# Two pads that move the large tiles of both ends of the on-chip memory to multiples of 512 bytes, and one rotation buffer less

## The chip, the cores and the metric

The kernel runs on one core of a Trainium2 chip. The core has TensorE (PE; its weight loads are shown apart, as PEld), VectorE (DVE), ScalarE (ACT), GpSimd (POOL) and SyncE (SP, which issues the DMAs). Its on-chip memory has 128 partitions; a tile takes the same range of bytes in each of them, and an address below is a byte offset within a partition. The metric is the device time of one execution, in microseconds (us).

## The reference

One inference step of a one-layer hybrid encoder, in float32, for 1024 new frames of one stream (the prompt) and 16 frames for each of 8 running streams (the samples), 1152 rows in all. After an RMSNorm one input projection feeds two groups of heads: a gated linear recurrence (RG-LRU) and a sparse attention whose keys are chosen by an indexer's top-k. Both meet in an output projection, and a SwiGLU feed-forward of width 2816 follows.

```python
h = rmsnorm(x, norm_mix);  proj = h @ w_in            # xr, gate, q, k, v, qi, ki, wi
xc, conv_new = causal_conv(xr, conv_prev, conv_w, conv_b)
hs, h_last = rglru(xc, pos, h_prev, ...);  y_a = hs * gelu(gate)
q = rope(rmsnorm(q, q_norm), pos);  k = rope(rmsnorm(k, k_norm), pos)
qi = rope(qi, pos);  ki = rope(ki, pos)
topk = min(256, k_all.shape[1] // 4)
y_b = dsa_attend(q, qi, wi, pos, k_all, v_all, ki_all, k_pos, topk)
x = x + concatenate([y_a, y_b], -1) @ w_out
gu = rmsnorm(x, norm_ffn) @ w_ffn_in
x = x + (silu(gu[..., :2816]) * gu[..., 2816:]) @ w_ffn_out
```

## The kernel before

The 1152 rows are nine tiles of 128. Every operand of a large product is split into a high and a low part, and a product is three matmuls (`mm3`, L245): low weights by high data, high weights by low data, high by high. Each matmul loads its own weights, a block of 128 x 128, and then moves 256 to 512 columns past them.

The stages follow one another in `build` (L266): norms and keys; the indexer's scores (`index`); the LRU, with the query projection (`q_proj`, L1203) woven into it; the LRU's half of the output projection (`out_tile_a`, L1339); attention; the other half of the output projection (`out_tile`, L1359); the feed-forward (`ffn`, L1624). The top-k counts run on DVE and ACT beside the stages from the indexer to `out_tile_a`. A planner with costs for each engine (`run`, L93) sets the order in which the streams of a stage are recorded, and a scheduler then orders each engine's instructions.

In the feed-forward two kinds of product alternate over 22 slices of the width. The first (`ffn1`) has weights of w_ffn_in in `w` and, in two of every ten half slices, in the spare tile `rest`; the moving data are the normed rows `hf`, 384 columns at a time. The second (`ffn2`) has the activations `a` as weights and moves 512 columns of w_ffn_out, which lie in `w` (pool tile `w2`) and, for one half slice in six, in `rest`. DVE adds its results into `acc`.

Memory is taken from both ends: pools with `side=L` are stacked from the bottom, pools with `side=R` from the top down. At the left lie `const` (L271, the identity and a constant) and the six large tiles of the pool `h` (L279), which serve in turn as `h`, `rest`, `smr`, `acc`, `smp` and `hf`. At the right come first `raw` (L275, two buffers for loads) and `wr` (L276, the eight slots named `w`), and then what each stage needs. In the LRU stage the two stacks meet: the lowest tile of the right stack begins where the left one ends.

A query half tile (`q_tile`, L1208) is a product of 24 matmuls, copied out to `qn` by ACT. Then `rope` (L496) runs: POOL makes two products of `qn` with a table into the ring tile `rp`, DVE multiplies `qn` by the other table in place, and DVE adds `rp`. There are 18 half tiles. `rope` takes the ring's size as `bufs`, with 2 as default; the index queries and the keys' rope already pass 1.

Of the kernel before, what the change touches and what calls it, by code (L numbers as in the profile page):

```python
# [9 lines left out]
F32 = mybir.dt.float32  # L10
# [71 lines left out]
class Kernel:  # L82
# [183 lines left out]
    def build(self, upto=99):  # L266
        ctx, tc, nc, I, O = self.ctx, self.tc, self.nc, self.I, self.O
        L = "left"
        R = "right"
        self.psum = ctx.enter_context(tc.tile_pool(name="psum", bufs=8, space=PSUM))  # L270
        self.const = ctx.enter_context(tc.tile_pool(name="const", bufs=1, side=L))  # L271
        self.dram = ctx.enter_context(tc.tile_pool(name="dram", bufs=1, space=bass.MemoryType.DRAM))
        right, yst, mid, tka, kist = (ExitStack() for _ in range(5))
        pool = lambda st, name, side, bufs=1: st.enter_context(tc.tile_pool(name=name, bufs=bufs, side=side))
        self.raw = pool(right, "raw", R, 2)  # L275
        self.wr = pool(right, "wr", R, self.SLOTS)  # L276
        yF_p = pool(yst, "yF", R)
# [930 lines left out]
    def q_tile(self, i, half, tp, gq):  # L1208

        nc = self.nc  # L1210
        w, = yield from self.wait_w(("q", half))
        tab = self.tables(tp, i, gq, 2)
        pq = self.ps()
        for d in range(ND):
            ww = w[d // 2]
            self.mm3(pq[:, :256], self.h_lhs(i, d, 0), self.h_lhs(i, d, 1), ww[:, d % 2, 0, :],
                     ww[:, d % 2, 1, :], d == 0, d == ND - 1)
        if i == NT - 1:
            self.wused -= 4
        self.n_q += 1  # L1220
        self.begin()
        x = self.qn[:, i, half * 256:half * 256 + 256]
        nc.scalar.activation(x, pq[:, :256], AF.Copy)
        t = self.end()
        for h in range(4):
            sq = tp.tile([128, 64], BF16, tag="sq", name="sq")
            nc.scalar.activation(sq, pq[:, h * 64:h * 64 + 64], AF.Square, scale=0.125,
                                 accum_out=self.qss[:, i, 4 * half + h:4 * half + h + 1])
        yield 0.0
        yield from self.until(t)  # L1230
        x = x.rearrange("p (h d) -> p h d", h=4)
        self.rope(x, x, tab, 4, tp)

    def q_norm(self, tp):

# [515 lines left out]
```

## Time and profile before

| | us |
|---|---|
| median of 3 runs (1546.99 to 1549.92) | 1549.23 |
| the profiled execution | 1549.64 |
| its span in the trace | 1547.9 |
| PE busy, by the page | 1479.1 |
| DVE, ACT, POOL busy | 866.1, 619.5, 269.3 |
| mean granted clock of PE, share of full speed | 0.978 |

The page lists busy times over the whole span; a share of it is an average over stages with different limits. The slices of the page show how the shares change along the span, and the view by stretches gives them for one stage. [...]

### The profile page before, as it was taken

Reading aid. Unit: us, or ns where it says so; the run is one execution under the profiler, and the core shown is the slowest. Engines: PE = TensorE matmul, PEld = TensorE weight load, DVE = VectorE, ACT = ScalarE, POOL = GpSimd, SP = SyncE. Lnnn points to the kernel's source line nnn. Section 1 sums busy time; section 2 is a strip of 40 time slices with the busy share of each in tenths; the row PEclk is TensorE's granted clock in tenths of the full one; section 3 lists DMA queues with packets and bytes.
Section 4 is the critical chain, followed back from the end, with each engine's and each line's share of the span. In section 5 each row is a group of like instructions: output and inputs, shape, how many; then the busy total and the mean of one; then the engine's idle time right before and its main releaser. Section 6 shows DMA issues by size and latency. Waiting matters only on the chain.

```text
span 1547.9 us, 20878 instructions
## 1 busy us (share of the span) xinstructions
PE 1479.1 (96%) x7786; PEld 1314.3 (85%) x7786; DVE 866.1 (56%) x1904; ACT 619.5 (40%) x1481; POOL 269.3 (17%) x425
## 2 busy tenths in 40 slices
PE   6889899889997999999999999999999999999998
PEld 6877688778745788889999898989898989898987
DVE  7556899899968987677233334242424242515133
ACT  5447988978315878655202020202121111111100
POOL 4214233334764545200000000000000000000000
PEclk8999899999998999999999999999999999999999
DMA  7201111011410002123102020202011111101003
GB/s 240 58 16 31 46 37 30 4 31 57 153 41 11 1 28 58 39 56 92 46 0 82 1 82 4 79 20 63 27 55 31 51 42 41 55 28 55 28 0 122
DMA packets 95093, 75.24 MB, mean 49 GB/s; under 512 B 13380, under 2 KB 85828, under 8 KB 94992
## 3 DMA queue, kind: packets, MB, share of 16 engines
q1 hardware_dynamic: 94992, 73.91, 15.8%
q8 instruction: 61, 1.00, 0.3%
q14 instruction: 40, 0.33, 0.1%
HBM read 67.62 MB, written 6.27 MB: 48 GB/s over the span
## 4 chain that ended last, share of the span: by engine, by line
PE 75%; DVE 10%; ACT 6%; issue 4%; POOL 2%; DMA 2%; SPq 0%; ACTq 0%; DVEq 0%; POOLq 0%
PE ps L207 68%; PE ps L212 4%; DVE junk L66 4%; PE ps L217 3%; ACT jk L66 3%; DVE tk_cand L66 2%; ACT L66 1%; DVE tr L66 1%; ACT tr L66 1%; DMA gk<-in_k_norm_dram 0%; ACT relu L66 0%; DMA x<-in_x_prompt_dram 0%; POOL m L66 0%; DVE s L66 0%; DVE m L66 0%
## 5 line engine op out<-in xcount | busy, mean ns | idle before, releaser
L207 PE MATMUL ps<-hf,w 128*128 128x384 f32 x2556 | 460.5, 338 | 0.0
L207 PEld LDWEIGHTS ps<-hf,w 128*128 128x128 f32 x2556 | 451.5, 187 | 0.8
L207 PE MATMUL ps<-w,a 128*128 128x512 f32 x999 | 239.1, 390 | 0.0
L66 DVE TENSOR_TENSOR acc<-ps,acc 128x512 f32<-128x512 f32 x234 | 161.0, 690 | 120.3 <-PE ps L207 119.2
L207 PEld LDWEIGHTS ps<-w,a 128*128 128x128 f32 x999 | 187.4, 188 | 40.1
L66 ACT ACTIVATE w<-raw 128x512 fp32r<-128x512 f32 x124 | 75.2, 628 | 300.5 <-PE ps L207 220.9
L66 DVE TENSOR_TENSOR sg<-ps,sg 128x384 f32<-128x384 f32 x66 | 36.7, 557 | 279.9 <-PE ps L207 279.3
L66 DVE TENSOR_TENSOR w<-raw,w 128x512 fp32r<-128x512 f32 x116 | 76.8, 687 | 85.2 <-ACT w L66 85.0
L66 ACT ACTIVATE a<-sg 128x384 fp32r<-128x384 f32 x66 | 34.5, 523 | 220.8 <-DVE sg L66 220.8
L207 PE MATMUL ps<-hf,rest 128*128 128x384 f32 x612 | 114.5, 334 | 0.0
L66 ACT ACTIVATE jk<-s,tk_cand 128x384 bf16<-128x384 f32 (+3 forms) x128 | 99.5, 777 | 32.4 <-DVE tk_cand L66 29.6
L207 PE MATMUL ps<-h,w 128*128 128x384 f32 x576 | 107.1, 343 | 0.0
L207 PEld LDWEIGHTS ps<-hf,rest 128*128 128x128 f32 x612 | 106.9, 188 | 0.2
L207 PEld LDWEIGHTS ps<-h,w 128*128 128x128 f32 x576 | 100.8, 188 | 3.9 <-ACT relu L66 0.2
L207 PE MATMUL ps<-w,h 128*128 128x256 f32 (+1 forms) x600 | 97.0, 318 | 0.0
L207 PEld LDWEIGHTS ps<-w,h 128*128 128x128 f32 x600 | 84.3, 192 | 6.6 <-issue 0.2
L66 ACT ACTIVATE sg<-ps 128x384 f32<-128x384 f32 x66 | 32.1, 486 | 122.0 <-PE ps L207 122.0
L212 PE MATMUL ps<-wa,yF 128*128 128x512 f32 x144 | 64.9, 605 | 2.7 <-DVE tk_cnt L66 2.7
L66 POOL TENSOR_SCALAR m<-m,mx 128x128 f32<-128x128 f32 (+7 forms) x64 | 51.7, 816 | 53.6 <-DVE mx L66 42.7
L212 PEld LDWEIGHTS ps<-wa,yF 128*128 128x128 f32 x144 | 27.1, 194 | 36.0 <-issue 30.3
L207 PE MATMUL ps<-smr,vhl 128*128 128x512 f32 x162 | 54.0, 418 | 2.3 <-ACT smr L66 1.4
L66 ACT ACTIVATE m<-m,mx 128x128 f32<-128x128 f32 (+7 forms) x64 | 49.3, 770 | 16.1 <-DVE mx L66 15.7
(266 smaller groups left out, 2142.0 us busy)
## 6 DMA issues: line engine op xcount, KB each, us to landing
raw<-in_w_ffn_in_dram SPq DMA_DIRECT2D x44, 512.0 KB, 4.8
raw<-in_w_ffn_out_dram SPq DMA_DIRECT2D x22, 512.0 KB, 3.6
raw<-in_w_in_dram SPq DMA_DIRECT2D x16, 512.0 KB, 5.0
out_dram<-acc SPq DMA_DIRECT2D x9, 512.0 KB, 2.6
x<-in_x_prompt_dram SPq DMA_DIRECT2D x8, 512.0 KB
acc<-in_x_prompt_dram SPq DMA_DIRECT2D x8, 512.0 KB
tab<-in_rope_dram SPq DMA_DIRECT2D x43, 64.0 KB, 1.8
wa<-in_w_out_dram SPq DMA_DIRECT2D x4, 512.0 KB
```

The lines of the kernel that those rows point to most:

```text
L66: return f(*args, **kw)
L207: self.nc.tensor.matmul(out, lhsT, rhs, start=start, stop=stop)
L212: self.nc.tensor.matmul(out, lhsT, rhs, start=start, stop=stop)
L217: self.nc.tensor.transpose(out, in_, self.ident[0:n, 0:n])
```

## The change

Two tiles that nothing reads or writes are taken ahead of the others: 88 floats (352 bytes) at the left end, behind which the tiles of `const` and `h` follow, and 120 floats (480 bytes) at the right end, ahead of `raw`. All that is stacked behind them moves. Room for it comes from the ring `rp` in the query stage, which has one buffer of 1024 bytes instead of two.

```diff
@@ -269,9 +269,11 @@
         self.const = ctx.enter_context(tc.tile_pool(name="const", bufs=1, side=L))
+        self.const.tile([128, 88], F32, name="pad_l")
         self.dram = ctx.enter_context(tc.tile_pool(name="dram", bufs=1, space=bass.MemoryType.DRAM))
         right, yst, mid, tka, kist = (ExitStack() for _ in range(5))
         pool = lambda st, name, side, bufs=1: st.enter_context(tc.tile_pool(name=name, bufs=bufs, side=side))
+        pool(right, "pad", R).tile([128, 120], F32, name="pad_r")
         self.raw = pool(right, "raw", R, 2)
         self.wr = pool(right, "wr", R, self.SLOTS)
@@ -1229,7 +1231,7 @@
         x = x.rearrange("p (h d) -> p h d", h=4)
-        self.rope(x, x, tab, 4, tp)
+        self.rope(x, x, tab, 4, tp, bufs=1)
```

In the built programs the tiles begin here (bytes in a partition, and what is left over from a multiple of 512):

| tiles | before | after |
|---|---|---|
| `h`, `rest`, `smr`, `acc`, `smp`, `hf` (first at) | 1696, over 160 | 2048, over 0 |
| `ki1`, `ki2` | 76960, 81568, over 160 | 77312, 81920, over 0 |
| the slots `w`, `wa`, `m` (first at), `raw` | 188384, 221152, over 480 | 187904, 220672, over 0 |
| `yF`, `a`, `w2`, `sg`, the scores `s` | over 480 | over 0 |
| `vhl`, `kn` | over 32 | over 64 |
| `k1`, `k2` | over 64 | over 96 |
| `qeo` of the index, `qn`, `relu` | over 352 | over 384 |
| tiles of the LRU: `bd`, `taps` / `xc`, `tr` | over 0 / over 256 | over 32 / over 288 |
| `ident` | over 128 | over 480 |

All of them are at multiples of 32 bytes before and after. The parts of a tile that one matmul takes lie at multiples of 512 bytes from its beginning in `h`, `hf`, `rest`, `w`, `w2` and `a`.

The order of instructions is the same on all engines but for a stretch from the end of the LRU to the end of `out_tile_a`. On POOL, in the query stage (`rp`, `tab` and `gq` belong to the query's rope, `tt`, `tr` and `yF` to the LRU), before:

```order
L66 TENSOR_TENSOR tab<-tab,gq 128x128
L66 TENSOR_TENSOR rp<-qn,tab 128x4x32 x4
L66 TENSOR_SCALAR tt<-tt 128x384 x3
L66 MEMSET tr 128x1
L66 TENSOR_TENSOR tab<-tab,gq 128x128
L66 MEMSET tt 128x8
L66 TENSOR_TENSOR rp<-qn,tab 128x4x32 x2
L66 TENSOR_TENSOR tab<-tab,gq 128x128
L66 TENSOR_TENSOR rp<-qn,tab 128x4x32 x2
L66 TENSOR_TENSOR yF<-yF,tr 128x384
```

and after:

```order
L66 TENSOR_TENSOR tab<-tab,gq 128x128
L66 TENSOR_TENSOR rp<-qn,tab 128x4x32 x2
L66 TENSOR_SCALAR tt<-tt 128x384 x3
L66 MEMSET tr 128x1
L66 TENSOR_TENSOR rp<-qn,tab 128x4x32 x2
L66 MEMSET tt 128x8
L66 TENSOR_TENSOR tab<-tab,gq 128x128
L66 TENSOR_TENSOR yF<-yF,tr 128x384
L66 TENSOR_TENSOR rp<-qn,tab 128x4x32 x2
L66 TENSOR_TENSOR tab<-tab,gq 128x128
```

The products of two half tiles that stood in a row are apart, and the first product of the LRU into `yF` has two half tiles less ahead of it. On DVE, at the first additions of `out_tile_a` (`acc`; `jk`, `ps`, `tk_cnt` belong to the top-k's masks, `tail` and `qss` to the query's norm), before:

```order
L66 TENSOR_TENSOR qss<-tail 128x72
L66 SCALAR_TENSOR_TENSOR ps<-jk_912 128x512
L66 SCALAR_TENSOR_TENSOR ps<-jk_912,ps 128x256
L66 TENSOR_TENSOR acc<-ps,acc 128x512
L66 TENSOR_TENSOR tk_cnt<-tk_cnt,ps 128x1
L66 TENSOR_TENSOR acc<-ps,acc 128x512
L66 TENSOR_TENSOR qn<-qn,tab 128x256
```

and after:

```order
L66 TENSOR_TENSOR qss<-tail 128x72
L66 SCALAR_TENSOR_TENSOR ps<-jk_917,ps 128x256
L66 TENSOR_TENSOR qn<-qn,tab 128x256
L66 TENSOR_TENSOR tk_cnt<-tk_cnt,ps 128x1
L66 TENSOR_TENSOR acc<-ps,acc 128x512
L66 TENSOR_TENSOR qn<-qn,rp 128x256
L66 TENSOR_SCALAR tk_cnt<-tk_cnt 128x1
L66 TENSOR_TENSOR acc<-ps,acc 128x512
```

A half tile's product with the table comes ahead of the first addition, and its addition of `rp` between the first and the second. Ahead of the first `acc` addition there are 15 products and 15 additions of `qn` before, 14 and 13 after.

## Rows read from the trace of the kernel before

**Rows 1.** The page: busy time of PE, and its slices.
```profile
PE 1479.1 (96%) x7786; PEld 1314.3 (85%) x7786; DVE 866.1 (56%) x1904; ACT 619.5 (40%) x1481; POOL 269.3 (17%) x425
...
PE   6889899889997999999999999999999999999998
...
PEclk8999899999998999999999999999999999999999
```
**Rows 2.** Stages: stretch, its length, busy us of each engine, granted clock, DMA, GB/s.
```profile
0.00:184.00 184.00, 156.94 (x785) 131.78 (x785) 122.09 (x254) 112.54 (x282) 62.66 (x120) 0.92 0.27 79
184.00:407.00 223.00, 206.41 (x1187) 185.74 (x1187) 206.53 (x551) 184.98 (x499) 82.16 (x131) 0.97 0.16 52
407.00:475.00 68.00, 65.33 (x160) 28.93 (x159) 46.12 (x103) 10.94 (x49) 40.90 (x70) 0.97 0.14 41
475.00:652.00 177.00, 159.19 (x985) 136.00 (x984) 147.57 (x428) 133.78 (x324) 83.54 (x104) 0.95 0.09 26
652.00:722.00 70.00, 69.84 (x361) 59.56 (x360) 53.20 (x112) 36.79 (x72) 0.00 (x0) 1.00 0.22 61
722.00:1543.00 821.00, 821.00 (x4316) 772.28 (x4315) 289.86 (x459) 140.49 (x262) 0.00 (x0) 1.00 0.15 45
```
**Rows 3.** PE's groups by form, 739.58 to 1543.28 us: output<-moving,weights; busy, mean ns.
```profile
L207 PE MATMUL ps<-hf,w 128*128 128x384 f32 x2413 | 435.2, 338 | 0.0
L207 PE MATMUL ps<-w,a 128*128 128x512 f32 x999 | 239.1, 390 | 0.0
L207 PE MATMUL ps<-hf,rest 128*128 128x384 f32 x612 | 114.5, 334 | 0.0
L207 PE MATMUL ps<-rest,a 128*128 128x512 f32 x189 | 54.2, 394 | 0.0
```
**Rows 4.** The same stretch in the view by stretches, columns as in rows 2.
```profile
739.58:1543.28 803.70, 803.70 (x4213) 754.70 (x4212) 278.53 (x440) 129.82 (x242) 0.00 (x0) 1.00 0.14 43
```
**Rows 5.** PE's timeline, the first slices of ffn1: start, length, instructions merged.
```profile
722.34 17.40 PE L207 MATMUL ps<-hf,w 128*128 128x384 f32 x99
739.58 2.25 PE L207 MATMUL ps<-hf,rest 128*128 128x384 f32 x12
741.66 6.52 PE L207 MATMUL ps<-hf,w 128*128 128x384 f32 x36
748.02 2.25 PE L207 MATMUL ps<-hf,rest 128*128 128x384 f32 x12
```
**Rows 6.** PE's timeline, ffn2 of the first slices and of the next.
```profile
790.22 24.64 PE L207 MATMUL ps<-w,a 128*128 128x512 f32 x108
814.70 4.40 PE L207 MATMUL ps<-hf,w 128*128 128x384 f32 x24
...
866.70 0.86 PE L207 MATMUL ps<-rest,a 128*128 128x512 f32 x3
867.40 2.22 PE L207 MATMUL ps<-w,a 128*128 128x512 f32 x9
869.46 0.86 PE L207 MATMUL ps<-rest,a 128*128 128x512 f32 x3
```
**Rows 7.** PE's timeline, the output projection's second half.
```profile
657.07 1.76 PE L207 MATMUL ps<-w,rest 128*128 128x512 f32 x7
658.67 0.86 PE L207 MATMUL ps<-smr,vhl 128*128 128x512 f32 x3
```
**Rows 8.** PE's wait in out_tile_a: timeline, and the stretches around it.
```profile
425.25 4.41 PE L212 MATMUL ps<-wa,yF 128*128 128x512 f32 x6 [2.67 <-DVE tk_cnt L66]
...
421.00:426.00 5.00, 2.33 (x7) 0.93 (x6) 4.96 (x11) 0.00 (x0) 4.64 (x7) 1.00 0.09 26
426.00:430.00 4.00, 4.00 (x7) 1.56 (x6) 3.62 (x7) 0.00 (x0) 4.00 (x4) 0.57 0.06 16
```
**Rows 9.** The ring tile `rp`, 355 to 430 us: durations min/median/max, and POOL's wait.
```profile
L66 POOL TENSOR_TENSOR rp<-qn,tab x24: 450/459/837, 367.4 to 424.0; 128x128 f32<-128x128 f32 x24
...
  POOL rp L66: 0.8, 1
```

## The prediction

> **What bounds the kernel now.** I read the page first, then the span cut into stages, then PE's groups by form and its timeline in the longest stage, and last the waits of the stage where instructions move. The page gives PE 1479.1 us of a 1547.9 us span, and its slices show PE at nine tenths or more from the middle of the span to the end, at a granted clock of nine tenths or more everywhere [rows 1]. [...] Before that, up to 722 us, PE shares the work: from 184 to 407 us DVE is busy 206.53 of 223 us and ACT 184.98.
>
> In the feed-forward stage only four kinds of matmul run, and their durations already differ by where the operands lie, at the same number of columns [rows 3]: 384 columns take 338 ns with weights in `w` and 334 ns with weights in `rest`; 512 columns take 390 ns with moving data in `w` and 394 ns in `rest`. These durations overlap, so the pace has to come from starts in the timeline. With weights in `rest`: 12 matmuls from 739.58 to 741.66, 2.08 us, 173.3 ns each. With weights in `w`: 36 from 741.66 to 748.02, 6.36 us, 176.7 ns each [rows 5]. For 512 columns, `w` moving and `a` as weights: 108 from 790.22 to 814.70, 24.48 us, 226.7 ns each; `rest` moving and `a` as weights: 3 from 866.70 to 867.40, 0.70 us, 233.3 ns each; and in that alternation the `w`,`a` matmuls themselves need 9 in 2.06 us, 228.9 ns [rows 6]. [...]
>
> Now the addresses of the built program. `hf` and `rest` stand on the left, 160 bytes past a multiple of 512; `w` and `a` on the right, 480 past. The two pairs with the shorter pace (`hf` with `rest`, `w` with `a`) have both operands at the same offset from a multiple of 512; the two with the longer pace (`hf` with `w`, `rest` with `a`) have them 192 bytes apart. In the changed program all four stand at offset 0. That is the only thing in the diff that reaches this stage.
>
> **The change part by part.** *The feed-forward stage.* From 739.58 to 1543.28 us there are 803.70 us [rows 4] with 2413 + 612 matmuls of 384 columns and 999 + 189 of 512 [rows 3]. If every pair takes the pace that equal offsets show, this is 3025 x 173.3 ns = 524.2 us and 1188 x 226.7 ns = 269.3 us, together 793.6 us: 10.1 us less. DVE and ACT, at 35% and 17% of the stage, stay hidden below PE, and so do the loads, which no PE gap waits for. [...]
>
> One set of rows speaks against a plain rule of offsets: from 722.34 to 739.58 us the same unequal pair, `hf` with `w`, runs 99 matmuls in 17.24 us, 174.1 ns each [rows 5]. The longer pace is then something into which the two reads fall, not a fixed price of the pair. It does not change the sum, since equal offsets show the shorter pace in all long groups that I divided.
>
> [...]
>
> *Before the feed-forward stage.* `w` with `rest` in the output projection (216 matmuls of 512 columns, 480 against 160) runs 7 matmuls in 1.60 us, 228.6 ns [rows 7]; at 226.7 this is 0.4 us, at the longer 233.3 it would be 1.4 us. PE is busy 69.84 of 70 us there [rows 2], so I take 0.7. The LRU and index projections (576 and 168 matmuls with 192 bytes or more between the operands) could give 576 x 3.4 ns + 168 x 6.6 ns = 3.1 us, or nothing, as DVE sets the pace there; in attention, `vhl` goes from offset 32 to 64 and `k1`, `k2` from 64 to 96, so these pairs stay unequal: between 0.6 us lost and 1.3 us gained on 216 matmuls, by +3 and -6 ns each. I take 0.3 for all of these, near the lower end, where DVE's 206.53 busy us put it.
>
> *The rotation buffer.* In the query stage each half tile lets POOL make two products into `rp` and DVE add `rp` in. With one buffer POOL's products of the next half tile wait for DVE's addition. The order shows this: POOL's four products in a row become two and two; on DVE a `qn` product now stands just ahead of the first addition into `acc`, while three `qn` operations that preceded that addition drop behind it. PE feels it at one place only: at 421.6 us it stops for a PSUM buffer that DVE's `acc` additions give back, 2.67 us of waiting, and takes 4.41 us for the next six matmuls at a granted clock of 0.57 [rows 8]. A gain is bounded by that wait, 2.7 us. The loss: 13 half tiles precede the addition, and each could hold DVE up by a POOL pair, 2 x 0.459 = 0.92 us, 12 us in all. In the trace of before, POOL waits for its own ring once, 0.8 us [rows 9], and DVE has other counts and masks to do between an addition and the next product; queued behind a waiting DVE are these masks and the `acc` additions, and PE waits for the latter alone. I take 0.3 us lost.
>
> Sum against the profiled execution, 1549.64 us (span 1547.9, 1.7 us around it), which lies 0.4 us above the median of the runs, 1549.23: 1549.64 - 10.1 - 0.7 - 0.3 + 0.3 = 1538.8 us.
>
> **The rivals.**
> 1. *The sides, not the offsets.* The pairs with the shorter pace are also those with both operands on one side of the memory: `hf`, `rest` left, `w`, `a` right. If distance is what counts, nothing changes in the stage: 1549.6 + 0.3 - 0.3, 1549.6 us, give or take 2. For it: no row has a cross pair at equal offsets. Against it: the cross pair at 174.1 ns [rows 5]; distance alone would not let it reach that.
> 2. *Start addresses do not matter* and the differences have another cause, such as which stage's state PE came from: again 1549.6 us. [...]
> 3. *One offset for everything is the worst case*, slower than before: with all large tiles at 0, each weight load and each moving read begins in step, and all pairs take the longer pace: 3025 x 176.7 + 1188 x 233.3 = 811.7 us, 8.0 more: 1557.6 us. It decides if `hf` with `rest`, now at 173.3, comes out at 176.7. Against it: equal offsets have the shorter pace now, twice.
> 4. *The single `rp` buffer is paid by PE*: if DVE loses 0.92 us on each of the 13 half tiles, PE's wait at 421.6 us becomes 15 us, and with rival 1 the end is at 1562; with the forecast's gain, at 1550.5. It outweighs the forecast's gain from about 11 us of added wait. The trace has only the 0.8 us for it.
> [...]
>
> **How the numbers follow.** Forecast 0.66 (its own range 1534 to 1543: the attention and LRU bounds below, the longer pace kept in some groups, and a few us of rotation wait above); rival 1 0.12; rival 2 0.07; rival 3 0.05; rival 4 0.06; rival 5 0.04. To hold 8 in 10 the range takes in the forecast and rivals 1 and 2 up to 1550: 1534 to 1550. A measurement of this kernel tells 0.2%, 3.1 us, from no change: faster means below 1546.1. The forecast (nearly all of it) and rival 5 give 0.70 and half of rival 4 with a gain left 0.02: 0.72. Rivals 1 and 2 without their edges give 0.17, the rest 0.11.
>
> **What would show it.** Right: in the feed-forward timeline all groups of 384 columns start 173.3 ns apart and all of 512 columns 226.7 ns; the durations of the four forms meet at 334 and 390 ns; the stage, from its first `hf` matmul of this kind to the last, is 10 us shorter, and the stages before 722 us end within 3 us of where they do. Wrong: `hf` with `w` still at 176.7 while its offsets are equal (rival 1), all forms at 338 and 394 ns (rival 3), a PE wait longer than 8 us before the second third of the `wa` matmuls (rival 4), or a pace below 170 ns (rival 5).

## The result, and the profile after

The changed kernel takes 1537.25 us (median of 6 runs, 1535.44 to 1538.64); the kernel before, timed beside it, 1547.15 us (6 runs, 1546.41 to 1549.92). The ratio is 0.993, with a 95% interval of 0.9918 to 0.9943: 9.9 us less. The forecast was 10.8 us less, from 1549.6 to 1538.8.

The page of the changed kernel, in the form of [rows 1]:

```profile
span 1535.1 us, 20876 instructions
...
PE 1467.9 (96%) x7786; PEld 1307.5 (85%) x7786; DVE 865.2 (56%) x1904; ACT 619.2 (40%) x1481; POOL 269.7 (18%) x425
```

PE's busy time fell by 11.2 us, the span by 12.8 (these two executions lie a little further apart than the medians); DVE, ACT and POOL each changed by less than 1 us. PE did the same 7786 matmuls in less time.

The feed-forward part, cut as in [rows 4] (columns: stretch, its length, busy us of PE, its weight loads, DVE, ACT and POOL, granted clock, DMA share, GB/s). In both kernels the cut is now at the start of the first `hf`,`rest` matmul and at the start of the last `w`,`a` matmul, first before, then after:

```profile
739.58:1543.02 803.44, 803.44 (x4213) 754.70 (x4212) 278.53 (x440) 129.82 (x242) 0.00 (x0) 1.00 0.14 43
```
```profile
736.32:1530.24 793.92, 793.92 (x4212) 747.20 (x4212) 278.76 (x440) 129.74 (x242) 0.00 (x0) 1.00 0.14 43
```

PE is busy without a gap in both, at a granted clock of 1.00 in both, and 9.52 us of the gain lie here. The groups of that stretch answer to [rows 3]:

```profile
L207 PE MATMUL ps<-hf,w 128*128 128x384 f32 x2413 | 427.8, 334 | 0.0
L207 PE MATMUL ps<-w,a 128*128 128x512 f32 x998 | 238.1, 389 | 0.0
L207 PE MATMUL ps<-hf,rest 128*128 128x384 f32 x612 | 114.3, 334 | 0.0
L207 PE MATMUL ps<-rest,a 128*128 128x512 f32 x189 | 53.1, 389 | 0.0
```

The 338 ns of `hf`,`w` became 334, which `hf`,`rest` had all along, and the 394 ns of `rest`,`a` met `w`,`a` at 389. (The last of the 999 `w`,`a` matmuls starts just past the end of the cut, so 998 are counted.) A duration of 334 ns is longer than the 173.3 ns from one start to the next, so the pace is read from the starts in PE's timeline (start, length, what ran, how many; consecutive matmuls of one kind share a row), as in [rows 5, 6]:

```profile
719.05 17.43 PE L207 MATMUL ps<-hf,w 128*128 128x384 f32 x99
736.32 2.24 PE L207 MATMUL ps<-hf,rest 128*128 128x384 f32 x12
738.40 6.40 PE L207 MATMUL ps<-hf,w 128*128 128x384 f32 x36
744.64 2.24 PE L207 MATMUL ps<-hf,rest 128*128 128x384 f32 x12
...
862.10 0.85 PE L207 MATMUL ps<-rest,a 128*128 128x512 f32 x3
862.79 2.20 PE L207 MATMUL ps<-w,a 128*128 128x512 f32 x9
864.83 0.84 PE L207 MATMUL ps<-rest,a 128*128 128x512 f32 x3
```

`hf`,`w`: 36 from 738.40 to 744.64, 6.24 us, 173.3 ns each, where it was 176.7. `rest`,`a` with the `w`,`a` after it: 12 from 862.10 to 864.83, 2.73 us, 227.5 ns each, where it was 2.76 us, 230.0 ns [rows 6].

The part ahead of the feed-forward ends 3.26 us earlier (739.58 to 736.32). Its one PE wait that the prediction watched [rows 8] reads, after:

```profile
423.79 2.84 PE L212 MATMUL ps<-wa,yF 128*128 128x512 f32 x6 [0.92 <-DVE acc L66]
```
```profile
421.00:426.00 5.00, 4.08 (x11) 1.57 (x10) 4.96 (x10) 0.00 (x0) 5.00 (x5) 1.00 0.05 15
426.00:430.00 4.00, 4.00 (x11) 1.77 (x10) 3.19 (x5) 0.00 (x0) 4.00 (x8) 1.00 0.07 19
```

The wait became 0.92 us from 2.67, and the six matmuls took 2.84 us instead of 4.41, at a granted clock of 1.00 where it had been 0.57. The experiments below show whether the change did this.

### The profile page after: what moved, and what is told of

Same layout as the page of the kernel before. It is cut to its first block, busy times and chain, and to the rows that moved or that the text cites. A ratio compares the mean times of both kernels' runs of the same rounds, so it can differ in the third digit from the quotient of the medians.

```text
span 1535.1 us, 20876 instructions
## 1 busy us (share of the span) xinstructions
PE 1467.9 (96%) x7786; PEld 1307.5 (85%) x7786; DVE 865.2 (56%) x1904; ACT 619.2 (40%) x1481; POOL 269.7 (18%) x425
## 4 chain that ended last, share of the span: by engine, by line
PE 72%; DVE 13%; ACT 6%; issue 5%; POOL 2%; DMA 1%; SPq 0%; ACTq 0%; DVEq 0%; POOLq 0%
PE ps L207 66%; DVE junk L66 4%; PE ps L217 3%; ACT jk L66 3%; PE ps L212 3%; DVE tk_cand L66 2%; DVE tr L66 1%; ACT L66 1%; POOL rp L66 1%; DVE ti L66 1%; DVE qn L66 1%; ACT tr L66 1%; DVE m L66 1%; ACT relu L66 1%; DVE s L66 1%
## 5 line engine op out<-in xcount | busy, mean ns | idle before, releaser
L207 PE MATMUL ps<-hf,w 128*128 128x384 f32 x2556 | 453.1, 334 | 0.0
L207 PEld LDWEIGHTS ps<-hf,w 128*128 128x128 f32 x2556 | 444.2, 188 | 0.7
L207 PE MATMUL ps<-k,qeo 128*128 128x384 f32 (+5 forms) x192 | 51.9, 383 | 3.7 <-DVE qeo L66 2.9
```

What stands on the lines that cost most here:

```text
L207: self.nc.tensor.matmul(out, lhsT, rhs, start=start, stop=stop)
```

## The experiments

The theory: a matmul's pace depends on where the moving data start against where the weights start, counted modulo some power of two, and the two pads make them agree. Its rivals: that the starts have to lie on multiples of 512; that the side of the memory counts; that the single rotation buffer moved the time. Below, "left" and "right" give the starts of the large tiles modulo 512 (`hf`, `rest` left; `w`, `a`, `w2` right; before 160 and 480, after 0 and 0). The rows leave numbers out of names: the `w` of `w`,`a` is the tile `w2`.

**One buffer, no pads.** The changed kernel without both pads.

```diff
-        self.const.tile([128, 88], F32, name="pad_l")
-        pool(right, "pad", R).tile([128, 120], F32, name="pad_r")
```

> No pads, one rp buffer: the tiles stand where they stood before (160 at the left, 480 at the right), the order of instructions is that of the changed kernel. If the gain in the feed-forward comes from the offsets, the feed-forward keeps its paces of before (176.7 and 173.3 ns for 384 columns, 226.7 and 233.3 ns for 512) and its 803.7 us. What the single buffer does shows in out_tile_a: the changed kernel ended that stage 1.5 us earlier and had no stretch of half clock at 426 us. If the single buffer's order did that, this kernel is 1 to 3 us faster than before; if the offsets did, it is within 1.5 us of before.

Measured: 1546.24 us over 12 runs, ratio to before 0.9996 (0.9985 to 1.0007). The feed-forward and the watched wait:

```profile
733.94:1537.38 803.44, 803.44 (x4213) 754.70 (x4212) 278.70 (x440) 130.00 (x242) 0.00 (x0) 1.00 0.14 43
```
```profile
419.89 4.54 PE L212 MATMUL ps<-wa,yF 128*128 128x512 f32 x6 [2.54 <-DVE acc L66]
```

803.44 us, as before to the hundredth, and the wait is 2.54 us, near the 2.67 of before. The single buffer neither gains nor costs what these runs can tell, and it does not make the wait short by itself.

**Equal, but not on a multiple of 512.** No left pad, a right pad of 320 bytes: left 160, right 160.

```diff
-        self.const.tile([128, 88], F32, name="pad_l")
-        pool(right, "pad", R).tile([128, 120], F32, name="pad_r")
+        pool(right, "pad", R).tile([128, 80], F32, name="pad_r")
```

> No left pad, a right pad of 320 bytes: all large tiles of both ends stand 160 bytes past a multiple of 512, so none is at a multiple of 64 or 512, and all are equal. Theory of equal offsets: the feed-forward runs at 173.3 and 226.7 ns throughout, 794 us, and the total is within 2 us of the changed kernel (ratio to before about 0.993). Rival, multiples of 512 (or of 64) are what counts: the paces stay at 173 to 177 and 227 to 233 ns as in before, feed-forward near 804 us, ratio near 0.999.

Measured: 1536.36 us (4 runs), ratio 0.9936 (0.9917 to 0.9954).

```profile
735.68:1529.60 793.92, 793.92 (x4212) 747.19 (x4212) 278.73 (x440) 129.87 (x242) 0.00 (x0) 1.00 0.14 43
```

The same 793.92 us as with everything at 0. The multiples of 512 are not what counts.

**On multiples of 64, but apart.** Left 0, right 320, 192 bytes apart modulo 512 like the kernel before.

```diff
-        pool(right, "pad", R).tile([128, 120], F32, name="pad_r")
+        pool(right, "pad", R).tile([128, 40], F32, name="pad_r")
```

> Left pad as in the change, right pad of 160 bytes: left tiles at offset 0, right tiles at 320, all at multiples of 64, but 192 bytes apart as before. Theory of equal offsets: the paces of before come back, 176.7 ns for most hf,w groups and 233.3 for rest,a, feed-forward 803 to 804 us, ratio near 0.999. Rival, multiples of 64 are what counts: 173.3 and 226.7 ns, feed-forward 794 us, ratio near 0.993.

Measured: 1547.76 us (10 runs), ratio 1.0 (0.9989 to 1.0011).

```profile
737.27:1540.71 803.44, 803.44 (x4213) 754.68 (x4212) 278.79 (x440) 129.80 (x242) 0.00 (x0) 1.00 0.14 43
```

Two kernels with different addresses and the same distance agree to 0.01 us, in either class (793.92 and 793.92 us, 803.44 and 803.44): at these places only the difference mattered.

**One side, made unequal.** In the changed kernel a pad between `w2` and `a` moves `w2` to 192 while `a` stays at 0; both are on the right. Everything else stays equal.

```diff
+            if f == 0:
+                fp.tile([128, 80], F32, name="pad_w", bufs=1)
```

> The changed kernel with an unused tile of 320 bytes between w2 and a in the feed-forward's pool: w2 stands at offset 192, a at 0, both on the right side of the memory; hf, w and rest stay at 0. Theory of equal offsets: w,a groups of 512 columns go from 226.7 to about 233 ns (999 matmuls, 6 us), rest,a and hf,w stay at 226.7 and 173.3; feed-forward about 800 us. Rival, the two sides of the memory are what counts: w,a are on one side and stay at 226.7, feed-forward 794 us.

Measured: 1544.0 us (10 runs), ratio 0.9979 (0.9969 to 0.9988), 6.75 us above the changed kernel.

```profile
737.00:1537.57 800.57, 800.57 (x4213) 747.09 (x4212) 278.86 (x440) 129.81 (x242) 0.00 (x0) 1.00 0.14 43
```
```profile
L207 PE MATMUL ps<-hf,w 128*128 128x384 f32 x2413 | 427.7, 334 | 0.0
L207 PE MATMUL ps<-w,a 128*128 128x512 f32 x999 | 244.5, 395 | 0.0
L207 PE MATMUL ps<-hf,rest 128*128 128x384 f32 x612 | 114.3, 334 | 0.0
L207 PE MATMUL ps<-rest,a 128*128 128x512 f32 x189 | 53.8, 392 | 0.0
```

A pair on one side took a longer pace when its starts differed: `w`,`a` went from 389 to 395 ns, its starts from 227.1 to 233.2 ns apart, and the stretch grew by 6.65 us. That ends the side of the memory as the cause. One miss: `rest`,`a`, whose own starts are still equal, went from 389 to 392 ns (starts 226.9 to 230.4 ns apart) although it was expected to stay; it runs in threes between nines of the slowed `w`,`a`.

**The distance itself.** Four kernels with the left at 0, which differ from the changed one in the right pad alone: left out (right 480, distance 32), 32 bytes (448, 64), 96 bytes (384, 128), 224 bytes (256, 256).

```diff
-        pool(right, "pad", R).tile([128, 120], F32, name="pad_r")
+        pool(right, "pad", R).tile([128, 8], F32, name="pad_r")
```

> Left tiles at 0, right tiles at 480 modulo 512: the two sides lie 32 bytes apart (modulo 512), one rope buffer. Theory 'only equal offsets are fast': hf,w 176.4 ns and rest,a 233 ns as in the kernel before, feed-forward 803.4 us from its first hf,rest matmul to its last. Rival 'the distance sets the price': near 0, little of it, so hf,w between 173.4 and 175 ns and the feed-forward 794 to 799 us. Either way the time is read from that stretch, since a whole run moves by 2 to 3 us.

> Left at 0, right at 448 modulo 512: 64 bytes apart. Theory 'only equal offsets are fast': 176.4 ns (hf,w), 233 ns (rest,a), feed-forward 803.4 us. Rival 'the distance sets the price': between the run at 32 bytes and the one at 128.

> Left at 0, right at 384 modulo 512: 128 bytes apart. Theory 'only equal offsets modulo 512 are fast': 803.4 us in the feed-forward. Rival 'equal modulo 128 (or a divisor of it that 192 misses) will do': 793.9 us.

> Left at 0, right at 256 modulo 512: 256 bytes apart. Theory 'only equal offsets modulo 512 are fast': 803.4 us in the feed-forward, hf,w 176.4 ns. Rival 'equal modulo 256 will do': 793.9 us and 173.4 ns. If the price grows with the distance, this is the dearest of the four, above 803.4 us.

One run each: 1550.89, 1542.82, 1548.34 and 1535.04 us, beside 1547.94 for the kernel before. Their feed-forward parts in the same order:

```profile
740.59:1544.19 803.60, 803.60 (x4212) 754.61 (x4212) 278.38 (x440) 129.91 (x242) 0.00 (x0) 1.00 0.14 43
```
```profile
738.23:1536.11 797.88, 797.88 (x4213) 748.29 (x4212) 278.37 (x440) 129.79 (x242) 0.00 (x0) 1.00 0.14 43
```
```profile
738.54:1541.63 803.09, 803.09 (x4213) 754.23 (x4212) 278.75 (x440) 129.90 (x242) 0.00 (x0) 1.00 0.14 43
```
```profile
734.43:1528.35 793.92, 793.92 (x4212) 747.26 (x4212) 278.70 (x440) 129.97 (x242) 0.00 (x0) 1.00 0.14 43
```

Worked out from all starts of each trace (mean distance from one start to the next, waits left out), in ns, with the changed kernel and the kernel before sorted in. The distance is left minus right, modulo 512; the two `hf` columns hold the matmuls that are followed by one of the same pair:

| distance | `hf`,`w` | `hf`,`rest` | `rest`,`a` | `w`,`a` | stretch, us |
|---|---|---|---|---|---|
| 0 (changed kernel) | 173.4 | 173.4 | 226.9 | 227.1 | 793.92 |
| 256 | 173.4 | 173.4 | 226.9 | 227.1 | 793.92 |
| 64 | 173.3 | 175.3 | 229.8 | 229.4 | 797.88 |
| 128 | 175.9 | 175.0 | 232.0 | 228.3 | 803.09 |
| 192 (before) | 176.6 | 173.5 | 233.3 | 227.8 | 803.44 |
| 32 | 176.5 | 173.4 | 234.2 | 228.1 | 803.60 |

Both theories missed. Equal modulo 512 is too strict, since 256 bytes apart is as good as 0. And the price does not grow with the distance: 32 bytes cost as much as 192, and 64 bytes cost `hf`,`w` nothing, though the whole stretch still loses 3.96 us against equal starts. Most of that is paid by pairs whose own two starts agree: 998 `w`,`a` at 2.4 ns more are 2.4 us, 612 `hf`,`rest` at 1.7 ns more in the mean of all are 1.1 us, and only 0.5 us is the unequal `rest`,`a`. For `hf`,`rest` the rows show it:

```profile
738.23 2.27 PE L207 MATMUL ps<-hf,rest 128*128 128x384 f32 x12
740.33 6.41 PE L207 MATMUL ps<-hf,w 128*128 128x384 f32 x36
746.58 2.27 PE L207 MATMUL ps<-hf,rest 128*128 128x384 f32 x12
```

12 in 2.10 us against 2.08 in the changed kernel. By place in the twelve, averaged over the 51 groups of this run, the first four take 184.5, 175.6, 181.5 and 173.4 ns, and then 173.3 to the end. So here this pair lost its time in the first three matmuls after the distance changed; `w`,`a` behind `hf`,`w` was slow in its first three as well, 229.2, 232.2 and 231.1 ns, and at 227 from then on.

**Other places, and both buffers.** The kernel before with one pad of 64 bytes: left 160, right 416, 256 apart. Once with one rotation buffer, and once with two, for which room comes from another reserve.

```diff
+        pool(right, "pad", R).tile([128, 16], F32, name="pad_r")
...
-        self.rope(x, x, tab, 4, tp)
+        self.rope(x, x, tab, 4, tp, bufs=1)
```
```diff
+        pool(right, "pad", R).tile([128, 16], F32, name="pad_r")
...
-    nc = _bacc.Bacc("TRN2", target_bir_lowering=False, num_devices=1, dynamic_dma_scratch_size=1024)
+    nc = _bacc.Bacc("TRN2", target_bir_lowering=False, num_devices=1, dynamic_dma_scratch_size=512)
```

> The kernel before with one pad of 64 bytes on the right and one rope buffer: left tiles at 160, right tiles at 416 modulo 512, so 256 bytes apart as in the run d256, but at other places. Theory 'the two starts must agree modulo 256': feed-forward 793.9 us, median within 1.5 us of the changed kernel's 1537.2. Rival 'modulo 512, and the run at 256 bytes apart owed its pace to tiles at 0 and 256': feed-forward 803.4 us, median about 1546.

> [...] All large tiles lie as in the kernel with one rope buffer. If the single buffer costs nothing, the two medians agree within 1.5 us; if the wait for it is paid somewhere, this one is faster by that. Expected: 1536 to 1538 us for both.

Measured: 1538.08 us with one buffer (5 runs, ratio 0.9934, 0.9922 to 0.9947) and 1537.86 us with two (5 runs, 0.9931, 0.9917 to 0.9945). First one buffer, then two:

```profile
737.43:1531.35 793.92, 793.92 (x4212) 747.20 (x4212) 278.62 (x440) 129.86 (x242) 0.00 (x0) 1.00 0.14 43
```
```profile
736.76:1530.68 793.92, 793.92 (x4212) 747.20 (x4212) 278.53 (x440) 129.87 (x242) 0.00 (x0) 1.00 0.14 43
```

Of the distances tried (0, 32, 64, 128, 192, 256) the stretch has its shortest time at those that are equal modulo 256, at 0 and 256 as at 160 and 416. The second buffer is worth 0.2 us, within the spread. The gain of the change could be had with 64 bytes in place of 832. No version was faster than the changed kernel by more than the measurement tells.

## Why the prediction was right

**The feed-forward term, -10.1 us.** Measured 9.52 us of the 9.9. That step held: the pairs with unequal starts came to the paces that the equal pairs had shown. The forecast time of the stretch was 793.6 us and it takes 793.92. The 0.3 us are a matter of size: the means are 173.4 and 227.0 ns where 173.3 and 226.7 were read off single groups, 0.8 us more, and the sum had two matmuls more than there are starts between the cuts, 0.4 us. The rest of the difference is on the side of before: its 803.70 us ran 0.26 us past the start of the last matmul, and 803.44 us lie between the starts.

**Which weights the pace goes with.** In the kernel before, `hf`,`rest` runs in twelves, of which the first eleven take 173.2 to 173.7 ns and the last 175.7 ns (means over 51 groups). What differs for the last is that the next matmul's weights come from `w`. And an `hf`,`w` matmul that is followed by one with `rest` takes 173.3 ns, against 176.6 for the others. The weight loads of the same trace fit this: those of the `hf`,`w` run begin at 741.49 us, together with the last `hf`,`rest` matmul and one matmul ahead of their own, which starts at 741.66 [rows 5].

```profile
739.41 2.10 PEld L207 LDWEIGHTS ps<-hf,rest 128*128 128x128 f32 x12
741.49 6.37 PEld L207 LDWEIGHTS ps<-hf,w 128*128 128x128 f32 x36
```

So in this trace the pace of a matmul goes with the weights that are loaded beside it, those of the next: 175.7 ns where they come from `w` and 173.2 to 173.7 where they come from `rest` in the one pair, 176.6 and 173.3 in the other.

The 174.1 ns of `hf`,`w` ahead of 739.58, which the prediction held against a plain rule of offsets [rows 5], are a mean with one long start in it: the second matmul starts 257 ns after the first, and the other 98 take 16.98 us, 173.3 ns each, with their starts 192 bytes apart.

```profile
722.60 17.15 PE L207 MATMUL ps<-hf,w 128*128 128x384 f32 x98
```

All three kernels at distance 192 take 17.24 us for the 99; those with equal starts take 17.27 us, and those at 32 and 128 take 17.57 and 17.51 us. And at distance 32, where `hf`,`w` is slow nearly everywhere, one run of 144 takes 24.96 us, 173.3 ns each, and the next such run 25.44 us, 176.7 ns each:

```profile
891.24 25.12 PE L207 MATMUL ps<-hf,w 128*128 128x384 f32 x144
916.20 1.03 PE L207 MATMUL ps<-hf,rest 128*128 128x384 f32 x5
...
1066.84 25.60 PE L207 MATMUL ps<-hf,w 128*128 128x384 f32 x144
1092.28 1.07 PE L207 MATMUL ps<-w,a 128*128 128x512 f32 x4
```

So in these traces a pair with unequal starts took one of several paces, one of them that of equal starts. In the stretch of the kernel before 55 of the 57 `hf`,`w` runs take 176.7 ns in their first half and in their second, one run of 144 takes 174.7 in both, and one of 12 takes 175.0 and 174.6. The prediction said of these rows that the pace is not a fixed price of the pair, and that held; that it is something into which the two reads fall was its author's estimate, since the traces give the starts of matmuls and of weight loads and not the reads. In the changed kernel every `hf`,`w` run of the stretch settled at 173.3 ns within six matmuls. What chooses the pace when the starts are unequal is open.

Moving `w2` alone by 192 bytes cost 6.65 us with nothing else changed in the stretch. How the place of the weights acts on a matmul's pace, and why equality modulo 256 is enough, is not shown by any run.

**The output projection, -0.7 us, and the rest ahead of 722 us, -0.3.** The mean pace of `w`,`rest` fell from 230.0 to 227.7 ns: 216 x 2.3 = 0.5 us. The other groups hardly moved, as priced: `h`,`w` of 384 columns 174.4 to 173.6 ns, `smr`,`vhl` 232 to 233 in both, and `w`,`h` of 256 columns went the other way, 117.8 to 119.8 ns, which gives back 432 x 2 ns = 0.9 us where PE is the bound. The sum of these terms can't be told from the runs: of the 9.9 us, 0.4 us are left for them beside the feed-forward, less than whole runs can tell. The feed-forward begins at 736.27 us in the mean of six profiled executions with distance 0 or 256 up to there (734.43 to 737.43) and at 737.98 in that of five with 32, 128 or 192, among them before and the one-buffer kernel (733.94 to 740.59). The spread in either class is larger than the difference of 1.7 us, so the 3.26 us between the two traces compared above can't be put down to the change. They are also just outside the 3 us that the prediction named as a sign of being right, a sign that such a spread makes worthless. (Two slips in its reading of [rows 1] touch no number: the clock's slices show 8, not nine tenths, in three places, and PE's last slice is an 8.)

**The rotation buffer, +0.3 us.** Taken alone it moved the median by less than 1 us, and with two buffers against one at the same offsets by 0.2 us. Rival 4's wait beyond 8 us never appeared: over the profiles it was 0.59 to 3.20 us, whichever number of buffers. Its length went by when PE came to the `wa` matmuls against DVE: in the one-buffer kernel without pads PE began them at 402.48 us and DVE its first `acc` addition at 419.16, and PE waited 2.54 us; in the changed one they began at 408.00 and 423.06, and PE waited 0.92. The step that held is that the ring seldom stopped anyone: in the changed kernel, as in the nine others with one buffer, POOL waited for DVE's additions of `qn` twice in the whole run, 1.5 us in all, where the loss put as a bound was 13 times 0.92 us.

```profile
POOL rp L66 <- DVE qn L66: 1.5, 2, 1.0
```

**The rivals.** Sides of the memory (1): out by the run with `w2` moved. Addresses do not matter (2): out by the pair of runs at 160 with 160 and at 0 with 320; that something beside the pair counts as well, which this rival named, is so for the unequal pairs above (173.3 and 176.7 ns for the same pair at distance 32); whether it is a state of PE is not shown. Equal starts as the worst case (3) and a pace below 170 ns (5): out by the groups above, whose means in the kernels at 0 and 256 are 173.4 and 227.0 ns.

## What to carry to other kernels

Where PE runs without gaps, divide the stretch into pairs of moving tile and weight tile and compare their paces at equal columns; here 3.4 and 6.6 ns that went with the pair and not with the shape pointed to where the tiles start. Then try the moving tiles and the weights that are loaded beside them at starts equal modulo 256 bytes: at 384 and 512 columns this took 9.52 us from the stretch (64 bytes of pad, 0.6% of the time). Look at the distance, not at alignment to a round number: with all starts 160 past a multiple of 512 the stretch took the same 793.92 us as with all at 0. Read such a gain from the stretch, which here repeated to 0.01 us over five kernels, since the whole run scattered by 3 us and more.

## What the runs showed that was not expected

- Equal starts were not the best at every width: `w`,`h` with 256 columns takes 119.8 ns in the kernels at distances 0 and 256, and 117.8 in the kernel before, 117.5 in that at 64 and 118.3 in that at 32 (here the moving data lie right and the weights left).
- At distance 192 the first dozen matmuls of an `hf`,`w` run alternate, 177.4 and 175.8 ns by turns (means by place over the 53 runs of 24 or more); at distance 64 they settle at 173.3 within a few. Here a pair's pace was a pattern in time, and its mean said little about one matmul.
- `smr`,`vhl` in attention stays at 231 to 233 ns for 512 columns in every kernel. `vhl` moves otherwise than `w`: its starts equal those of `smr` only in the kernel at distance 64, where both are at 0, and the pace there is 231.5 ns. What holds it there, 5 ns above the feed-forward's pace, is open.
